# Modulation columns with two places and in written order on VectorE; low products last and U2 copied first in the passage to the up projection

## The chip, the core and the metric

The kernel runs on one core of a Trainium2 chip. The core has a matrix engine (TensorE, PE in the profile), three engines that work on vectors (VectorE or DVE, ScalarE or ACT, GpSimd or POOL), and SyncE (SP), which here only issues transfers. The engines run beside each other, each takes its own queue in order, and they wait for one another by semaphores. On-chip data lie in SBUF, the results of PE in PSUM. The metric is the time of one execution on the device in microseconds (us), lower is better.

## The reference, cut to what matters

One layer of a diffusion backbone is applied to 128 context tokens and 512 grid tokens; the kernel treats them as 640 columns of one matrix.

```python
def trunk_layer(x, cvec, lw, ...):
    mod = jax.nn.silu(cvec) @ lw['w_ada'] + lw['b_ada']            # 1024 -> 6 * 1024
    sh1, sc1, g1, sh2, sc2, g2 = jnp.split(mod, 6, axis=-1)
    h = rmsnorm(x, lw['norm1_g']) * (1.0 + sc1) + sh1
    mix, kh, vh, s_f, s_b = token_mixers(h, ...)     # short conv, HGRN2, attention, gMLP, gates, w_o
    x = x + g1 * mix
    h = rmsnorm(x, lw['norm2_g']) * (1.0 + sc2) + sh2
    x = x + g2 * conv_ffn(h, lw['w_up'], lw['ffn_conv_w'], lw['ffn_conv_b'], lw['w_down'])
    return x, kh, vh, s_f, s_b

def conv_ffn(h, w_up, cw, cb, w_down):
    z = dwconv3(h @ w_up, cw, cb)
    a, g = jnp.split(z, 2, axis=-1)
    return (jax.nn.silu(g) * a) @ w_down
```

`cvec` has two rows, one for the grid tokens and one for the context. All is float32. The result is `rmsnorm` of both outputs, with the keys, values and final HGRN2 states of the context.

## The kernel before

**Precision.** A float32 product is made of three passes of PE over a narrower type: each operand is split into a high half (a copy by ACT) and a low half (the rest, by a subtraction on DVE), and PE adds high times high, high times low and low times high. The weight of each product thus has a high and a low half, and so has the activation. Where `low_dma` is used, the low half is made by ACT (a negated copy) and an accumulating transfer that POOL issues.

**Order of the work.** Weight tiles go through a list of units; for each, the transfer is issued four units ahead, the split two ahead, and the products follow. Beside these run jobs, written as Python generators: HGRN2, gMLP, convolution, attention and the modulation columns. A clock of planned PE time counts up with each product (`tick`), and when a job's time has come it writes its next few instructions and yields how much planned time to wait; `drain` runs all jobs until a named result has been written. A planner then orders each engine's queue: among instructions whose inputs are ready by its own reckoning it takes the one written first, so an instruction that is ready early can be issued ahead of what was written before it. `tc.keep_in_program_order` ties an instruction behind the one written just before it for the same engine. In the gates in pairs and the up projection the switch `fixed` does that for all of DVE, ACT and POOL.

**Modulation.** Its first 16 blocks of 128 outputs are made by PE at the start. The other 32 are columns: `ada_cols` loads the 128 x 1024 weights of one block f (`w_adt`, 512 KB, L244) and DVE multiplies them with `silu(c)` of each of the two rows and sums along the way (L248, twice a column). Columns 16 to 39 run beside the mixer stage (g1, shift 2, scale 2), columns 40 to 47 beside the down projection (g2). Each column is loaded into the one region H, where its second multiplication also leaves its scraps, so a load waits for the column before it. `HD[4]` is the planned time between a load and its multiplications, `HD[5]` after each multiplication. No new column starts while HGRN2's tail is written, from "hgrn_out" to "hgrn_done"; in that tail PE transposes ten blocks (L648) and DVE multiplies each out of PSUM (L652).

**HGRN2 on DVE.** Seven levels of products, each with elementwise steps on DVE (L558, L544), copies on ACT (L510) and POOL, and small matmuls (L538). Weight splits of the mixer stage are L347/L348 and L334/L335.

**The passage to the up projection.** The up projection works in 22 pairs, each with seven products (`prod`, L1411) in a scheme that saves one of eight; product numbers and operands are in `PROD`. Product i takes 4 blocks of 128 with three passes, 12 matmuls. Products 1 and 2 of the first four pairs (`BRIDGE`, `up_start`) run while the second norm is finished (`norm2`); then `operands` makes the sums of activations for the others (operand 5 in region B, 6 in A, 7 in D, operand 3 in XL1) and `up_pair` carries on. Pairs 2 and 3 of the bridge get their low weights by `low_dma`. Products 6 and 5 of a pair go to two banks of one PSUM tile; product 6's bank is copied out by ACT (U2, `tmp`) before product 7 adds to it. All instructions of these helpers bear line L131, except matmuls.

**The down projection.** L1722 multiplies in two halves of 11 tiles; between them `down_out` scales with g2, and x from the stage before is read back into X0, X1 and G. Region X1 holds the convolution's results in the up projection; the last pair's are stored to `actd` from there.

Of the kernel before, what the change touches and what calls it, by code (L numbers as in the profile page):

```python
# [12 lines left out]
AF = mybir.ActivationFunctionType  # L13
# [1 line left out]
AX = mybir.AxisListType  # L15

P = 128
HD = [4, 5, 2.1, 7, 4.4, 1.4, 1.5, 5, 2.0, 2, 11]
NE = [lambda p, v: p, lambda p, v: v]
OUTS = 1  # L20
NPAIR = 22
BRIDGE = 4
# [7 lines left out]
HC = 320  # L30
# [20 lines left out]
def tile_step(ctx: ExitStack, tc: tile.TileContext, a: dict, outs: list, dbg=None):  # L51
# [178 lines left out]
    gcol = const.tile([P, 2, 2, 8], F32, name="gcol")  # L230
    growd = dram.tile([2, 16, P], F32, name="growd")

    def ada_cols(fs, tag="S0"):

        cr = region(tag, [P, 2, D])
        cf = cr.rearrange("p v c -> p (v c)")
        nc.sync.dma_start(cf, a["cc"].rearrange("v c -> (v c)").partition_broadcast(P))
        act(cf, cf, AF.Silu)
        for f in fs:
            while "hgrn_out" in R and "hgrn_done" not in R:  # L240
                yield 1
            raw = region("H", [P, D])
            junk = gp.tile([P, D], mybir.dt.bfloat16, tag="gt", name=nm("junk"))
            nc.sync.dma_start(raw, a["w_adt"][f - 16])  # L244
            yield HD[4]
            ar = sp.tile([P, 2], F32, tag="red", name=nm("ar"))
            for v in range(2):
                vec.scalar_tensor_tensor(raw if v else junk, raw, 1.0, cr[:, v], ALU.mult, ALU.mult,  # L248
                                         accum_out=ar[:, v:v + 1])
                yield HD[5]  # L250
            if f // 8 in (2, 5):
                vec.tensor_scalar(gcol[:, f // 8 // 5, :, f % 8], ar, p1[:, C_BADA + f:C_BADA + f + 1],
                                  None, ALU.add)
                if f % 8 == 7:
                    gain_rows(f // 8 // 5)
            else:
                modulate(f, ar)
        R["ada%d" % f] = True

    def gain_rows(i):  # L260

# [144 lines left out]
    def evac_in(sec, n, ps):  # L406
        psv = None if isinstance(ps, list) else ps[:, :, 0:HC]
        if sec in ("ff", "fb"):
            d = 0 if sec == "ff" else 1
            ff = need("A", "FF", [P, 2, 2, T])  # L410
            kk = need("B", "KK", [P, 2, 2, T])
            if psv is None:
                for c in range(2):
                    cs = slice(c * HC, (c + 1) * HC)
                    act(ff[:, d, n, cs], ps[c], AF.Sigmoid)
                    act(kk[:, d, n, cs], ps[c], AF.Sigmoid, scale=-1.0)
            else:
                act(c2(ff[:, d, n]), psv, AF.Sigmoid)
                act(c2(kk[:, d, n]), psv, AF.Sigmoid, scale=-1.0)
            i = d * 2 + n  # L420
            vec.tensor_scalar(ff[:, d, n], ff[:, d, n], oml[:, i:i + 1], lb[:, i:i + 1],
                              ALU.mult, ALU.add)
            vec.tensor_scalar(kk[:, d, n], kk[:, d, n], oml[:, i:i + 1], None, ALU.mult)
        elif sec == "q":
            dd = need("D", "HD", [P, 2560])
            act(c2(dd[:, n * T:(n + 1) * T]), psv, AF.Silu)
        elif sec == "g":
            o = need("MG1", "HO", [P, 2560])
            act(c2(o[:, 1280 + n * T:1280 + (n + 1) * T]), psv, AF.Silu)
        elif sec == "du":  # L430
            x0 = need("X0", "DX0", [P, 2560])
            act(c2(x0[:, n * T:(n + 1) * T]), psv, AF.Copy)
        elif sec in ("ac", "ax", "ab"):
            if (sec, n) == ("ac", 0):
                drain(lambda: "hgrn_out" in R)
            y = need("MG0", "YA", [P, 2, 2, T])
            if sec == "ac":
                act(c2(y[:, 0, n]), psv, AF.Copy)
                return
            if sec == "ab":  # L440
                drain(lambda: "conv" in R)
            x = y[:, 0 if sec == "ax" else 1, n]
            vec.tensor_tensor(c2(x), psv, c2(x), ALU.mult)
            if (sec, n) == ("ab", 1):
                R["ya"] = split_y("A", y[:, 1].rearrange("p n t -> p (n t)"))
        elif sec in ("ck", "cq", "cv"):
            if sec == "cv":
                dst = need("G", "CG", [P, 1280])[:, n * T:(n + 1) * T]
            else:
                f = need("F", "CF", [P, 2560])  # L450
                o = 0 if sec == "ck" else 1280
                dst = f[:, o + n * T:o + (n + 1) * T]
            sc = 0.125 if sec == "cq" else 1.0
            cg, cw = (4, 16) if sec == "cq" else (8, 8)
            dv = dst[:, 0:TS].rearrange("p (g r c) -> p r g c", g=cg, r=8)
            for (b, r0, r1) in ((0, 0, 5), (1, 5, 8)):
                src = ps[:, b, 0:(r1 - r0) * 64].rearrange("p (r g c) -> p r g c", g=cg, c=cw)
                act(dv[:, r0:r1], src, AF.Copy, scale=sc)
            act(dst[:, TS:T], ps[:, 1, 192:320], AF.Copy, scale=sc)
# [435 lines left out]
    def in_tile(sec, n, w):  # L895
        ps = pg()
        gemm(ps, w, 0, 8, xhk, xlk)
        evac_in(sec, n, ps)
        if n == 1:
            R[sec + "_done"] = True  # L900
        if n == 1 and sec in starts:
            start(starts[sec](), 1.5, SLACK[sec])
            if sec == "q":
                start(ada_cols(range(16, 40)), HD[7])

    def tok_tile(sec, kh, w):

# [493 lines left out]
            oact(c[:, i], x, AF.Copy)  # L1401
            low_dma(c[:, 2 + i].rearrange("p b c -> p (b c)"), x.rearrange("p b c -> p (b c)"))

    def prod(o, p_, i, first):
        u, ih, il = PROD[i]
        wh = up[p_, u][:, ih]
        wl = up[p_, "C" if i == 7 else u][:, il]
        xh_, xl_ = fx["x"][i]
        for k in range(4):
            for j, (w, x) in enumerate(((wh, xh_), (wh, xl_), (wl, xh_))):  # L1410
                mm(o, w[:, k, :], x[:, k, :], start=(first and k == 0 and j == 0),  # L1411
                   stop=(k == 3 and j == 2), skip_group_check=True)
            tick(0.44)

    def up_start(p_):

        if p_ == 2 or p_ == 3:
            up[p_, "b"] = [pm()[:, 0:HC], None]
        else:
            g = pg()  # L1420
            up[p_, "b"] = [g[:, 0, 0:HC], g[:, 1, 0:HC]]
        prod(up[p_, "b"][0], p_, 1, True)
        if p_ >= BRIDGE:
            first_copy(p_)
        b3 = up[p_, "b3"] = pm()[:, 0:HC]
        prod(b3, p_, 2, True)
        if p_ < BRIDGE - 1:
            first_copy(p_)
            first_sum(p_)
# [58 lines left out]

    S2 = ((0, 192, 321), (192, HC, 514))

    def up_pair(p_, r):


        n, q, o = p_ + 1, p_ - 1, p_ - 2
        inner, nx = p_ < NPAIR, n < NPAIR
        if o >= 0:
            taps(o, 1)
        if q >= 0:
# [30 lines left out]
        if q >= 0:  # L1529
# [7 lines left out]
            if p_ == 1:  # L1537
                first_copy(3)
                first_sum(3)
        if inner:  # L1540

            if up[p_, "b"][1] is None:
                up[p_, "b"][1] = pm()[:, 0:HC]
            b1, b2 = up[p_, "b"]
            prod(b1, p_, 6, False)
            oact(tmp(p_ % 2), b1, AF.Copy)
        if q >= 0:

            prod(up[q, "b"][1], q, 3, False)
# [5 lines left out]
        if nx:  # L1555
            up_bl(n)
        if inner:
            prod(b2, p_, 5, True)
            prod(b1, p_, 7, False)

# [32 lines left out]
    def up_all(_):  # L1593
        fx["x"] = {1: (hh[0][:, 0], hh[0][:, 1]), 2: (hh[0][:, 2], hh[0][:, 3])}
        r1 = {1: up_load1(1)}
        drain(lambda: "n2_2" in R)
        for p_ in range(BRIDGE):
            if p_ + 1 < BRIDGE:
                up_a(p_ + 1, r1[p_ + 1])
            if p_ + 2 < BRIDGE:  # L1600
                r1[p_ + 2] = up_load1(p_ + 2)
            up_start(p_)
            if p_ == 1:
                drain(lambda: "n2_3" in R)
                operands(0, 192)
            if p_ == 2:
                up_b(0)
                up_bl(0)
        drain(lambda: "n2_4" in R)
        r = {0: first}  # L1610
        operands(192, HC)
        operand3()
        r[1] = up_load(1)
        fixed[0] = True
        for p_ in range(NPAIR + 1):
            up_pair(p_, r)
        fixed[0] = False
        taps(NPAIR - 1, 1)
        gate(NPAIR - 1)
        gated(NPAIR - 1)  # L1620
        keep(NPAIR - 1)
        start(ada_cols(range(40, 48), "MG1"))

    units.append((lambda: None, lambda pr: up_first(), up_all))

# [65 lines left out]
    def down_tile(nh, kk_, ws):  # L1691
        if (nh, kk_) == (0, 3):
            x2[0:2] = [x2r("X0")[:, 0:1024], x2r("X0")[:, 1024:2048]]
            x2[4] = x2r("G")[:, 0:1024]
        if (nh, kk_) == (0, 10):
            x2[2:4] = [x2r("X1")[:, 0:1024], x2r("X1")[:, 1024:2048]]
        if kk_ == 0:
            if nh == 0:
# [10 lines left out]
                return  # L1709
            batch = acc["hold"]  # L1710
        last = kk_ == 10
        if (nh, kk_) == (0, 10):
            drain(lambda: "ada47" in R)
            grows["g2"] = gain_load(1, "S0")
        for t in range(5):

            halves = ((0, 256), (256, 512)) if nh == 1 and t == 4 else ((0, 512),)
# [284 lines left out]
```

## Time and profile before

| | |
|---|---|
| median of 3 runs | 1060.93 us (1059.95 to 1065.95) |
| profiled execution, its own time | 1062.54 us |
| its span, first to last instruction | 1060.8 us |
| mean granted PE clock | 0.987 |
| PE busy | 1030.6 us, 97% of the span |
| DVE busy | 795.8 us, 75% |
| ACT busy | 521.0 us, 49% |
| POOL busy | 119.3 us, 11% |

The stages by time from the span's start: modulation of the first norm and first sections to about 60 us; the other sections with HGRN2, convolution and attention to 315; gates to 560; output projection and second norm to 626, up projection to 906, down projection to the end. A line of the profile names the line of the kernel, the engine, the operation, and the tile written and read (`m<-XH,MG`: from XH and MG into m); in brackets stands how long the engine had been idle before, and what ended that. PE counts as busy while matmuls are in flight. The granted clock says which share of PE's full rate it was allowed.

### The profile page before, as it was taken

Reading aid. Unit: us, or ns where it says so; the run is one execution under the profiler, and the core shown is the slowest. Engines: PE = TensorE matmul, PEld = TensorE weight load, DVE = VectorE, ACT = ScalarE, POOL = GpSimd, SP = SyncE. Lnnn points to the kernel's source line nnn. Section 1 sums busy time; section 2 is a strip of 40 time slices with the busy share of each in tenths; the row PEclk is TensorE's granted clock in tenths of the full one; section 3 lists DMA queues with packets and bytes.
Section 4 is the critical chain, followed back from the end, with each engine's and each line's share of the span. In section 5 each row is a group of like instructions: output and inputs, shape, how many; then the busy total and the mean of one; then the engine's idle time right before and its main releaser. Section 6 shows DMA issues by size and latency. Waiting matters only on the chain.

```text
span 1060.8 us, 18792 instructions
## 1 busy us (share of the span) xinstructions
PE 1030.6 (97%) x7648; PEld 968.3 (91%) x7648; DVE 795.8 (75%) x1278; ACT 521.0 (49%) x890; POOL 119.3 (11%) x151
## 2 busy tenths in 40 slices
PE   7998999989999999999999998999999999999997
PEld 6698988989999999999998888999999999888886
DVE  6568698868877486776775787998888887776834
ACT  6252235324243354454453287777777677533532
POOL 1013011021100000000010022212211111000201
PEclk9998999999999999999999999999999999999999
DMA  9663433445226222422244268865666668984212
GB/s 373 230 218 104 123 106 114 128 128 167 76 75 216 73 92 83 150 69 81 90 154 144 100 178 169 197 163 145 154 159 162 171 153 217 354 287 159 80 40 100
DMA packets 53863, 158.73 MB, mean 150 GB/s; under 512 B 7792, under 2 KB 16400, under 8 KB 51728
## 3 DMA queue, kind: packets, MB, share of 16 engines
q1 hardware_dynamic: 42416, 132.47, 37.2%
q0 software_dynamic: 11360, 25.05, 11.2%
q8 instruction: 60, 0.98, 0.4%
q14 instruction: 27, 0.22, 0.1%
HBM read 126.80 MB, written 16.80 MB: 135 GB/s over the span
## 4 chain that ended last, share of the span: by engine, by line
PE 91%; DVE 3%; ACT 2%; DMA 2%; issue 1%; POOL 1%; SPq 0%; POOLq 0%; ACTq 0%; DVEq 0%
PE g L1411 20%; PE g L382 19%; PE m L1112 14%; PE g L1722 8%; PE m L1722 6%; PE m L1411 5%; PE g L1125 4%; PE m L1248 3%; PE g L1248 2%; PE g L924 1%; PE g L1824 1%; PE m L538 1%; PE m L211 1%; DMA MG<-raw 1%; PE m L864 1%
## 5 line engine op out<-in xcount | busy, mean ns | idle before, releaser
L382 PE MATMUL g<-XH,w 128*128 128x320 f32 x832 | 205.6, 321 | 0.0
L382 PEld LDWEIGHTS g<-XH,w 128*128 128x128 f32 x832 | 144.9, 191 | 3.8 <-issue 2.4
L382 PE MATMUL g<-XL,w 128*128 128x320 f32 x416 | 130.3, 313 | 0.0
L382 PEld LDWEIGHTS g<-XL,w 128*128 128x128 f32 x416 | 79.7, 192 | 0.2 <-issue 0.2
L335 DVE TENSOR_TENSOR w<-raw,w 128x1024 fp32r<-128x1024 f32 x34 | 41.5, 1221 | 18.0 <-ACT w L334 17.3
L334 ACT ACTIVATE w<-raw 128x1024 fp32r<-128x1024 f32 x34 | 35.8, 1053 | 24.5 <-PE g L1248 16.1
L1722 PE MATMUL g<-w,XH 128*128 128x512 f32 (+1 forms) x216 | 47.5, 372 | 0.0
L1722 PEld LDWEIGHTS g<-w,XH 128*128 128x128 f32 x216 | 38.5, 188 | 7.3 <-DVE X L131 0.2
L1112 PE MATMUL m<-XH,w 128*128 128x320 f32 x192 | 45.0, 309 | 0.0
L348 DVE TENSOR_TENSOR w<-raw,w 128x1024 fp32r<-128x1024 f32 (+1 forms) x29 | 41.4, 1426 | 3.9 <-ACT w L347 3.8
L347 ACT ACTIVATE w<-raw 128x1024 fp32r<-128x1024 f32 (+1 forms) x29 | 32.4, 1118 | 17.6 <-issue 6.6
L131 DVE SCALAR_TENSOR_TENSOR X<-MG,p2t,X 128x641 f32<-128x641 f32 x44 | 38.9, 884 | 2.1 <-ACT X L131 1.2
L1722 PE MATMUL m<-w,XH 128*128 128x512 f32 (+1 forms) x180 | 40.3, 368 | 0.0
L1722 PE MATMUL g<-w,XL 128*128 128x512 f32 (+1 forms) x180 | 40.1, 373 | 0.0
L248 DVE SCALAR_TENSOR_TENSOR junk<-H,S 128x1024 bf16<-128x1024 f32 x24 | 31.4, 1309 | 11.5 <-DMA H<-in_w_adt_dram 11.5
L131 DVE SCALAR_TENSOR_TENSOR X<-X,p2t,X 128x641 f32<-128x641 f32 x44 | 38.9, 884 | 1.2 <-ACT X L131 0.3
L1411 PE MATMUL g<-XL,C 128*128 128x320 f32 x240 | 38.7, 310 | 0.1
L1411 PE MATMUL g<-XL,w 128*128 128x320 f32 x240 | 38.8, 310 | 0.0
L1722 PEld LDWEIGHTS g<-w,XL 128*128 128x128 f32 x180 | 32.2, 188 | 6.8 <-DVE dt L1733 0.6
L1411 PEld LDWEIGHTS g<-XL,C 128*128 128x128 f32 x240 | 35.9, 188 | 1.0 <-ACT MG L131 0.8
L1411 PEld LDWEIGHTS g<-XL,w 128*128 128x128 f32 x240 | 35.9, 188 | 0.7 <-ACT MG L131 0.3
L1722 PEld LDWEIGHTS m<-w,XH 128*128 128x128 f32 x180 | 31.3, 189 | 5.3
(513 smaller groups left out, 2719.7 us busy)
## 6 DMA issues: line engine op xcount, KB each, us to landing
raw<-in_w_up_dram SPq DMA_DIRECT2D x35, 512.0 KB, 5.1
H<-in_w_adt_dram SPq DMA_DIRECT2D x32, 512.0 KB, 3.5
raw<-in_w_gp_dram SPq DMA_DIRECT2D x18, 640.0 KB, 3.9
raw<-in_w_in_dram SPq DMA_DIRECT2D x22, 512.0 KB, 4.4
raw<-in_w_down_dram SPq DMA_DIRECT2D x22, 512.0 KB, 3.6
actd<-X POOLq DMA_DIRECT2D x22, 320.5 KB, 5.4
G<-in_w_up_dram SPq DMA_DIRECT2D x11, 512.0 KB, 4.8
raw<-in_w_gate_dram SPq DMA_DIRECT2D x8, 640.0 KB, 3.9
```

Of the source, the lines that this page charges most:

```text
L131: r = f(*args, **kw)
L248: vec.scalar_tensor_tensor(raw if v else junk, raw, 1.0, cr[:, v], ALU.mult, ALU.mult, accum_out=ar[:, v:v + 1])
L334: act(w[0], raw, AF.Copy)
L335: vec.tensor_tensor(w[1], raw, w[0].bitcast(F32), ALU.subtract)
L347: act(w[:, 0], raw, AF.Copy)
L348: low = lambda: vec.tensor_tensor(w[:, 1], raw, w[:, 0].bitcast(F32), ALU.subtract)
L382: mm(o, w[:, h, k0 + k, :], r(k)[:, s], start=(k == 0 and i == 0), stop=(k == kt - 1 and i == 2))
L1112: mm(o, w[:, k, :], x[:, k, :], start=(first and k == 0 and j == 0), stop=(k == 3 and j == 2), skip_group_check=True)
L1125: mm(pb[:, c, 0:HC], w[:, h + k, :], y[:, x, k, s], start=(k == 0 and j == 0), stop=(k == 1 and j == 2))
L1248: mm(m, mh[k // 2][:, hx, k % 2, t * P:(t + 1) * P], wo[q][:, hw, k % 2, :], start=(k == 0 and i == 0), stop=(k == 7 and i == 2))
L1411: mm(o, w[:, k, :], x[:, k, :], start=(first and k == 0 and j == 0), stop=(k == 3 and j == 2), skip_group_check=True)
L1722: mm(acc[nh][t + c0 // 256][:, 0:c1 - c0], sl[k][hx][:, t * P:(t + 1) * P], w[:, hw, k, c0:c1], start=(kk_ == 0 and k == 0 and i == 0), st ...
```

## The change

1. A column's place is now chosen by a function, and there are two in turn. In the mixer stage even columns go to H; odd ones to the free half of DX0 (region X0) until HGRN2's totals are written, then to region A, which is free by then. In the down projection odd columns go to H and even ones to a part of region X1.
2. The next column's load is written before this column's multiplications. Both multiplications are tied behind what was written before them on DVE.
3. The planned time of a column is 2.2 (mixer) or 5 (down) after its multiplications, instead of 4.4 before them. The pause for HGRN2's tail is looked at after that time.
4. Before region A is used for the split of the convolution's result, all columns to 39 must have been written. In the down projection the drain for column 47 and the load of g2 stand ahead of x's reload into X1.
5. In the first four pairs the high weights' eight matmuls of products 1 and 2 come first, then the four of each with the low weights.
6. For pair 0, product 6 and its copy out (U2) are written ahead of operand 3's split, which is written in `up_pair` now, after the load of pair 1.

```diff
-HD = [4, 5, 2.1, 7, 4.4, 1.4, 1.5, 5, 2.0, 2, 11]
+HD = [4, 5, 2.1, 7, 2.2, 1.4, 1.5, 5, 2.0, 2, 11]
...
-    def ada_cols(fs, tag="S0"):
+    def ada_cols(fs, tag, homes, gap):
...
+        raws = {}
+
+        def load(f):
+            if f in fs and f not in raws:
+                raws[f] = homes(f)
+                nc.sync.dma_start(raws[f], a["w_adt"][f - 16])
+
+        load(fs[0])
+        yield HD[4]
         for f in fs:
-            while "hgrn_out" in R and "hgrn_done" not in R:
-                yield 1
-            raw = region("H", [P, D])
+            load(f + 1)
+            raw = raws.pop(f)
             junk = gp.tile([P, D], mybir.dt.bfloat16, tag="gt", name=nm("junk"))
-            nc.sync.dma_start(raw, a["w_adt"][f - 16])
-            yield HD[4]
             ar = sp.tile([P, 2], F32, tag="red", name=nm("ar"))
             for v in range(2):
-                vec.scalar_tensor_tensor(raw if v else junk, raw, 1.0, cr[:, v], ALU.mult, ALU.mult,
-                                         accum_out=ar[:, v:v + 1])
+                tc.keep_in_program_order(
+                    vec.scalar_tensor_tensor(raw if v else junk, raw, 1.0, cr[:, v], ALU.mult, ALU.mult,
+                                             accum_out=ar[:, v:v + 1]))
                 yield HD[5]
...
-        R["ada%d" % f] = True
+            yield gap
+            while "hgrn_out" in R and "hgrn_done" not in R:
+                yield 1
+        R["ada%d" % fs[-1]] = True
+
+    def col_home(f):
+
+        if f % 2 == 0:
+            return region("H", [P, D])
+        if "tots" not in R:
+            return need("X0", "DX0", [P, 2560])[:, 1280:1280 + D]
+        return need("A", "A2", [P, 2560])[:, 0:D]
...
             if (sec, n) == ("ab", 1):
+                drain(lambda: "ada39" in R)
                 R["ya"] = split_y("A", y[:, 1].rearrange("p n t -> p (n t)"))
...
-                start(ada_cols(range(16, 40)), HD[7])
+                start(ada_cols(range(16, 40), "S0", col_home, HD[4]), HD[7])
...
-    def prod(o, p_, i, first):
+    def prod(o, p_, i, first, part=None):
...
-        for k in range(4):
+        for k in range(4) if part is not None else ():
+            for j, (w, x) in enumerate(((wl, xh_),) if part else ((wh, xh_), (wh, xl_))):
+                mm(o, w[:, k, :], x[:, k, :], start=(first and not part and k == 0 and j == 0),
+                   stop=(part == 1 and k == 3), skip_group_check=True)
+                tick(0.147)
+        for k in range(4) if part is None else ():
...
-        prod(up[p_, "b"][0], p_, 1, True)
         if p_ >= BRIDGE:
+            prod(up[p_, "b"][0], p_, 1, True)
             first_copy(p_)
         b3 = up[p_, "b3"] = pm()[:, 0:HC]
-        prod(b3, p_, 2, True)
+        if p_ >= BRIDGE:
+            prod(b3, p_, 2, True)
+        else:
+            for part in range(2):
+                prod(up[p_, "b"][0], p_, 1, True, part)
+                prod(b3, p_, 2, True, part)
...
+    def up_u2(p_):
+
+        if up[p_, "b"][1] is None:
+            up[p_, "b"][1] = pm()[:, 0:HC]
+        b1 = up[p_, "b"][0]
+        prod(b1, p_, 6, False)
+        oact(tmp(p_ % 2), b1, AF.Copy)
+
     def up_pair(p_, r):
...
+        if p_ == 0:
+            up_u2(p_)
+            operand3()
...
-        if inner:
-
-            if up[p_, "b"][1] is None:
-                up[p_, "b"][1] = pm()[:, 0:HC]
-            b1, b2 = up[p_, "b"]
-            prod(b1, p_, 6, False)
-            oact(tmp(p_ % 2), b1, AF.Copy)
+        if inner and p_:
+            up_u2(p_)
...
         operands(192, HC)
-        operand3()
         r[1] = up_load(1)
...
-        start(ada_cols(range(40, 48), "MG1"))
+        def down_home():
+            if "col" not in fx:
+                fx["col"] = region("X1", [P, 2560])
+            return fx["col"][:, 0:D]
+
+        start(ada_cols(range(40, 48), "MG1", lambda f: region("H", [P, D]) if f % 2 else down_home(), 5))
...
         if (nh, kk_) == (0, 10):
+            drain(lambda: "ada47" in R)
+            grows["g2"] = gain_load(1, "S0")
             x2[2:4] = [x2r("X1")[:, 0:1024], x2r("X1")[:, 1024:2048]]
...
-        if (nh, kk_) == (0, 10):
-            drain(lambda: "ada47" in R)
-            grows["g2"] = gain_load(1, "S0")
```

1 line of the change is left out of this document (added).

## The prediction

> **What bounds the kernel now.** I read the page's busy line first, then the span cut into stages, then the waits of TensorE (PE), and only then single stretches in order of time. The page and three rows of the stages (columns: length, PE busy, PEld, DVE, ACT, POOL, granted clock, DMA share, GB/s):
>
> ```profile
> PE 1030.6 (97%) x7648; PEld 968.3 (91%) x7648; DVE 795.8 (75%) x1278; ACT 521.0 (49%) x890; POOL 119.3 (11%) x151
> ...
> 92.00:104.00 12.00, 9.15 (x55) 8.94 (x54) 10.59 (x16) 2.88 (x6) 1.68 (x1) 0.72 0.31 94
> 152.00:159.00 7.00, 5.05 (x98) 4.71 (x97) 7.00 (x12) 1.89 (x3) 1.15 (x1) 0.76 0.34 99
> 159.00:220.00 61.00, 61.00 (x668) 58.30 (x668) 49.73 (x102) 26.95 (x62) 11.60 (x10) 1.00 0.39 122
> 220.00:232.00 12.00, 8.03 (x48) 7.69 (x47) 8.85 (x21) 0.00 (x0) 0.00 (x0) 0.86 0.42 131
> 619.00:650.00 31.00, 25.54 (x161) 24.26 (x160) 25.29 (x43) 25.23 (x46) 10.22 (x23) 0.94 0.96 200
> ```
>
> PE is the bound. No PE work is removed by the change, so all it can do is fill or open holes in PE's time. Within the body of the kernel four stretches have holes: 2.85 us idle in 92-104, 1.95 in 152-159, 3.97 in 220-232 and 5.46 in 619-650. Each also costs clock: 12.00 x (1 - 0.72) = 3.4 us, 7.00 x 0.24 = 1.7, 12.00 x 0.14 = 1.7, 31.00 x 0.06 = 1.9. What ended the holes:
>
> ```profile
> PE m L648 <- DVE MG L652: 4.0, 1, 4.0
> PE g L924 <- ACT E L928: 2.9, 1, 2.9
> PE g L1411 <- ACT MG L131: 2.6, 1, 2.6
> PE m L538 <- issue: 1.9, 1, 1.9
> PE m L1411 <- DMA MG<-raw: 1.9, 1, 1.9
> ...
> DVE junk L248 <- DMA H<-in_w_adt_dram: 18.4, 13, 5.1
> ```
>
> Columns here: total, times, longest. The last line is VectorE's (DVE's): thirteen times its queue stood still because a modulation column (L248) had not landed in its one place, H.
>
> **The columns in the mixer stage.** The hole of 220-232, on DVE and then on PE:
>
> ```profile
> 222.07 1.22 DVE L348 TENSOR_TENSOR w<-raw,w 128x1024 fp32r<-128x1024 f32 x1
> 225.35 1.23 DVE L248 SCALAR_TENSOR_TENSOR junk<-H,S 128x1024 bf16<-128x1024 f32 x1 [2.06 <-DMA H<-in_w_adt_dram]
> ...
> 226.62 1.75 DVE L652 SCALAR_TENSOR_TENSOR MG<-m,p1t,MG 128x128 f32<-128x128 f32 x5
> ...
> 227.02 0.47 PE L648 MATMUL m<-cst,MG 128*128 128x128 f32 x1 [3.97 <-DVE MG L652]
> ```
>
> PE cannot make another transpose (L648) until L652 has emptied a PSUM buffer, and L652 sits behind a column that waits 2.06 us for its transfer and takes 1.23. With two places the next column is loaded one column ahead (L244 before L248), so the wait goes; with the denser pace (5.0 us of planned PE time a column, 2.2 + 2 x 1.4, for 7.2 before) the columns that were late here have run earlier, and between hgrn_out and hgrn_done no new one is written. If the weight split (222.07) stays in front, L652 starts at 223.3 for 226.62: 3.3 us. The clock then isn't lost; of its 1.7 us I take 1.4, since a short wait for L652's release (five tiles of two, 0.35 each) remains. Gain 4.7 us, bounds 0 and 3.97 + 1.7 = 5.7.
>
> [...]
>
> What it costs: more columns in the same time, and each tied behind what is written before it on DVE, so that none floats up into idle time. All DVE work in 130-205, then L248's share of it (columns: length, DVE busy and count, clock, DMA):
>
> ```profile
> 130.00:205.00 75.00, 67.73 (x137) 0.98 0.36 111
> ...
> 130.00:205.00 75.00, 22.18 (x36) 0.98 0.36 111
> ```
>
> The x36 are 18 multiplications with their accumulator reads, so 9 columns of 22.18 / 9 = 2.46 us, one each 8.3 us. At the written pace there would be 75 / 5.0 = 15: 6 more, 14.8 us, for 75 - 67.73 = 7.3 us of idle time. So DVE overruns by up to 7.5 us, and HGRN's DVE steps slip by that. The cover is PE's other tiles: in 159-220 PE is busy 61.00 of 61.00 us while DVE is busy for 49.73. I take 0 for it, and keep 0 and 7.5 for the range; if the cover goes, see the third rival.
>
> In 92-104 the hole ends with an ACT copy that waits for HGRN's L558 on DVE, with a column ahead of it:
>
> ```profile
> 74.14 1.23 DVE L248 SCALAR_TENSOR_TENSOR junk<-H,S 128x1024 bf16<-128x1024 f32 x1 [5.15 <-DMA H<-in_w_adt_dram]
> ...
> 89.37 2.87 DVE L248 SCALAR_TENSOR_TENSOR junk<-H,S 128x1024 bf16<-128x1024 f32 x1
> ...
> 96.78 0.83 ACT L510 ACTIVATE D<-B 128x640 f32<-128x640 f32 x1 [5.69 <-DVE B L558]
> ```
>
> The first column floated up to 74.14, when DVE had nothing else to do. Tied behind HGRN's first steps it comes later, and I take it to stand where the second stands here. So 0; bounds: no column in the chain, all of 2.85 + 3.4 = 6.2 us won, or a second pair with it, 2.46 lost. The 1.95 us of "issue" have no releaser that the change touches: 0. On the SP queue each load stands one column earlier, and the weight loads behind it wait less: 0. The second place is free space in DX0 and then in A; the drain before A is split again finds all columns done, unless they stay at 8.3 us each: 0.
>
> **The passage to the up projection.** PE, with what it waits for, then the other engines:
>
> ```profile
> 627.87 0.46 PE L1411 MATMUL m<-XH,MG 128*128 128x320 f32 x2
> 630.23 3.49 PE L1411 MATMUL m<-XH,MG 128*128 128x320 f32 x22 [1.90 <-DMA MG<-raw]
> 633.56 3.72 PE L1411 MATMUL m<-XH,w 128*128 128x320 f32 x24
> 637.97 0.41 PE L1411 MATMUL g<-A,E 128*128 128x320 f32 x1 [0.70 <-ACT A L131]
> 643.13 3.49 PE L1411 MATMUL g<-B,E 128*128 128x320 f32 x12 [2.55 <-ACT MG L131]
> ...
> 633.83 0.49 DVE L131 TENSOR_TENSOR MG<-m,s 128x320 f32<-128x320 f32 x1 [1.28 <-PE m L1411]
> 634.24 1.22 DVE L131 TENSOR_TENSOR E<-S,E 128x1024 fp32r<-128x1024 f32 x1
> ...
> 632.33 1.05 ACT L131 ACTIVATE E<-S 128x1024 fp32r<-128x1024 f32 x1
> 639.40 1.27 ACT L131 ACTIVATE XL<-X 128x1280 fp32r<-128x1280 f32 x1 [0.30 <-DVE X L131]
> 642.66 0.41 ACT L131 ACTIVATE MG<-g 128x320 f32<-128x320 f32 x1
> ...
> 637.65 1.29 POOL L131 DMA_DIRECT2D B<-X  x1 [1.24 <-DVE X L131]
> ...
> B<-X POOLq DMA_DIRECT2D x1, 256.0 KB, 5.0
> ```
>
> Low products last: pair 2 now has 16 products that need no low weight, at (633.56 - 630.23) / 22 = 0.15 us each 2.4 us, where it had 2. From 627.87 they reach 630.3, and the transfer landed at 630.2: the 1.90 us wait goes. But PE only comes sooner to the next wait, for the operand of product 6 in A (637.97). That chain shortens by what DVE loses at 633.83: pair 2 ends before DVE asks for it, so E's low half starts when ACT has its high half, 632.33 + 1.05 = 633.4, instead of 634.24; I take 0.9 (bounds 0 and 1.28). U2 copied first: product 5 waits for the copy of product 6's bank (642.66 + 0.41 = 643.07), which stands on ACT behind operand 3 and four other copies; now it runs at once. Then the low half of operand 5 decides: 637.65 + 5.0 = 642.65, or 641.75 with the 0.9. So product 5 starts 1.4 us earlier (bounds 0.5 and 1.9). Of the 1.9 us of clock I take 0.5: a hole of some 1.9 us remains, 1.90 lost no clock at 630, 1.95 did at 153. Operand 3 and the copies to C come 0.4 us or more later on ACT, with POOL's transfers for them; a later stall on their low halves, or on the next pair's sums on DVE, is the lower end, 0.5 lost. Sum 1.9 us, bounds -0.5 and 1.9 + 1.9 = 3.8.
>
> **The columns in the down projection.** Even columns now go to X1, which is free only when the last pair's output has been stored:
>
> ```profile
> 915.97 0.54 POOL L131 DMA_DIRECT2D actd<-X  x1 [12.46 <-DVE X L131]
> ...
> 919.62 1.23 DVE L248 SCALAR_TENSOR_TENSOR junk<-H,MG 128x1024 bf16<-128x1024 f32 x1 [3.21 <-ACT MG L238]
> 920.77 1.22 DVE L335 TENSOR_TENSOR w<-raw,w 128x1024 fp32r<-128x1024 f32 x1
> ...
> 928.78 5.60 PE L1722 MATMUL g<-w,XH 128*128 128x512 f32 x24
> ...
> raw<-in_w_down_dram SPq DMA_DIRECT2D x5, 512.0 KB, 6.2
> H<-in_w_adt_dram SPq DMA_DIRECT2D x2, 512.0 KB, 4.3
> actd<-X POOLq DMA_DIRECT2D x1, 320.5 KB, 5.9
> ```
>
> Store and load end at 915.97 + 5.9 + 4.3 = 926.2, 6.6 us after the first column's start of before, and SP's queue stands at that load meanwhile. Behind the column on DVE is a weight split (920.77) that I read as due at the tile of 928.78: 926.2 + 1.23 + 1.22 = 928.6, just in time. Later columns catch up, since two can be in flight; x2's reload into X1, now behind the drain, comes while PE works on the last tile of the first half and is asked for after it. I take 0, bounds 0 and 3.8: with 6.2 for store and load alike the split ends at 915.97 + 12.4 + 2.45 = 930.8, 2.1 late, and a hole can take 1.7 of clock.
>
> [...]
>
> **Sum.** 4.7 + 1.9 = 6.6 us. The profiled execution took 1062.54 us (span 1060.8), 1.6 above the median of 1060.93: it would become 1055.9, and the median 1054.3.
>
> **Rivals.** (1) The hole only moves: HGRN's tail slips on the fuller DVE, or a column is still in front of L652, and the 4.7 stay; the passage alone gives 1060.9 - 1.9 = 1059.0. For it: 7.3 us of idle time for up to 14.8 of work. Against: the 20 us before 220 have no PE hole.
> (2) The place in X1 comes late: 1054.3 + 3.8 = 1058.1. Against: DVE's later work has slack.
> (3) Slower: the denser columns on DVE in 130-205. It decides once PE runs out of tiles whose splits are ready: then the 7.5 us of overrun come through to PE, with two half-clock windows of 1.7 as in 92-104, and the hole of 220-232 stays: 1060.9 - 1.9 + 7.5 + 3.4 = 1069.9. Against: PE's 61.00 of 61.00.
> (4) Better: the column leaves the chain of 92-104: 1054.3 - 6.2 = 1048.1.
>
> **How the numbers follow.** The forecast has 0.50, with its own range 1051 to 1058; (1) 0.14, (2) 0.08, (3) 0.17, (4) 0.11. Half a per cent, 5.3 us, is about what a measurement tells from no change: faster is below 1055.6, slower above 1066.2. Of the forecast's 0.50, 0.36 lie below 1055.6: faster 0.36 + 0.11 = 0.47; same 0.14 + 0.14 + 0.08 = 0.36; slower 0.17. The range 1048 to 1066.5 leaves out most of (3) and part of (4), 0.17 together.
>
> **What would show it.** Right: no line for L648 waiting on L652 above 1 us, DVE's waits for columns near 0, the clock at 1.00 in 220-232, the wait on MG<-raw gone, product 5 right after operand 5's transfer. Wrong: waits of PE on DVE in 104-220, DVE idle before the first column in X1 with PE idle at the tile after it, or a new stall at the second pair of the up projection.

## The result and the profile after

The changed kernel took 1066.89 us in the median of 13 runs (1063.63 to 1069.14), the kernel before 1061.69 beside it (1059.67 to 1066.09, 13 runs): ratio 1.0042, 95% interval 1.0026 to 1.0057. By the ratio it is some 4.5 us slower (5.2 between the medians), less than half a per cent, where I had forecast 6.6 us less. It lies 0.4 us above my range.

The profiled execution took 1066.1 us with a span of 1064.3. Its busy line and four stretches of the span (columns as in the prediction: length, PE, PEld, DVE, ACT, POOL, granted clock, DMA share, GB/s):

```profile
PE 1034.0 (97%) x7648; PEld 970.4 (91%) x7648; DVE 790.8 (74%) x1278; ACT 520.5 (49%) x890; POOL 122.3 (11%) x151
...
130.00:159.00 29.00, 25.61 (x602) 23.94 (x601) 27.24 (x49) 11.41 (x23) 5.23 (x4) 0.89 0.41 129
220.00:232.00 12.00, 11.94 (x89) 11.48 (x88) 9.60 (x20) 4.28 (x7) 0.00 (x0) 1.00 0.42 146
300.00:372.00 72.00, 68.82 (x473) 67.37 (x472) 34.09 (x42) 24.95 (x31) 0.00 (x0) 0.98 0.34 113
619.00:660.00 41.00, 35.22 (x216) 33.45 (x215) 32.67 (x60) 32.85 (x65) 12.47 (x26) 0.92 0.89 194
```

The same stretches of before that the prediction did not show:

```profile
130.00:159.00 29.00, 26.87 (x616) 24.98 (x615) 27.70 (x47) 10.21 (x23) 4.66 (x4) 0.94 0.31 98
300.00:372.00 72.00, 72.00 (x509) 70.34 (x509) 44.29 (x64) 27.14 (x33) 0.00 (x0) 1.00 0.39 134
619.00:660.00 41.00, 35.39 (x226) 33.84 (x225) 33.74 (x56) 32.74 (x58) 11.93 (x25) 0.96 0.91 197
```

For each stretch I add PE's idle time and the clock that was lost (length times one minus the granted clock). 220-232: 3.97 + 1.68 before, 0.06 after, 5.6 us won. 130-159: 2.13 + 1.74 before, 3.39 + 3.19 after, 2.7 lost. 300-372: nothing before, 3.18 + 1.44 after, 4.6 lost. 619-660: 5.61 + 1.64 before, 5.78 + 3.28 after, 1.8 lost. Together 3.5 lost, as much as the spans differ (1064.3 and 1060.8). That is a match of the large pieces and no exact account: the first section's products began 2.1 us earlier in this execution (57.68 for 59.77), by chance in what precedes the change, and some 2 us more are spread over pieces too small to name.

So the hole that I had priced was closed, and a new one of nearly the same size had opened 120 us later. PE's waits after:

```profile
PE g L1436 <- DMA B<-X: 3.7, 1, 3.7
PE g L400 <- ACT gt L984: 3.2, 1, 3.2
PE g L943 <- ACT E L947: 3.1, 1, 3.1
...
PE m L557 <- issue: 1.5, 1, 1.5
...
PE m L557 <- DVE C L577: 1.1, 1, 1.1
```

The second line is the new one. It belongs to the gates: ACT makes a sigmoid (L984, L965 before) out of PSUM, and PE needs that place for the next product. ACT's queue there, in the kernel before:

```profile
343.46 0.80 ACT L965 ACTIVATE gt<-g,p1t 128x640 f32<-128x640 f32 x1 [5.78 <-PE g L382]
347.47 0.42 ACT L131 ACTIVATE H<-raw 128x256 fp32r<-128x256 f32 x1 [3.21 <-DMA raw<-in_w_gp_dram]
```

and in the changed kernel, with PE's row below:

```profile
345.37 0.42 ACT L131 ACTIVATE H<-raw 128x256 fp32r<-128x256 f32 x1 [9.54 <-DMA raw<-in_w_gp_dram]
345.70 0.78 ACT L984 ACTIVATE gt<-g,p1t 128x640 f32<-128x640 f32 x1
...
346.53 0.42 PE L400 MATMUL g<-XH,w 128*128 128x320 f32 x1 [3.18 <-ACT gt L984]
```

The two rows of ACT have changed places. `H<-raw` is the weight copy of the first of the gates in pairs (`g_a`), and its destination is the region H, the columns' old home. Before, the last column held H until 336.9 us, so the planner wrote the copy behind the sigmoid. Now the last column in H is done at 257.5, and the copy stands one place ahead. But its source, a weight transfer, lands at 345 to 347 us in either kernel. ACT stands 9.54 us before the copy, and the sigmoid behind it, which needed nothing any more (PE's last product before its wait had ended at 343.34), comes late, at 345.70. Of the columns' last ends in H, the row

```profile
L248 DVE DVE_READ_ACCUMULATOR H<-H,S x24: 73/81/95, 78.1 to 336.9; 128x1 f32 x24
```

is the group of before whose last start is 336.9; the one after is

```profile
L255 DVE DVE_READ_ACCUMULATOR H<-H,S x12: 72/81/92, 100.1 to 257.5; 128x1 f32 x12
```

That the planner moved the copy because H was free is my reading of these ends; its reckoning is in no profile, though the run with the old pace below agrees with it. That the copy's place makes the hole was tested.

### The profile page after: what moved, and what is told of

Its sections match the earlier page's. It is cut to its first block, busy times and chain, and to the rows that moved or that the text cites. A ratio compares the mean times of both kernels' runs of the same rounds, so it can differ in the third digit from the quotient of the medians.

```text
span 1064.3 us, 18792 instructions
## 1 busy us (share of the span) xinstructions
PE 1034.0 (97%) x7648; PEld 970.4 (91%) x7648; DVE 790.8 (74%) x1278; ACT 520.5 (49%) x890; POOL 122.3 (11%) x151
## 4 chain that ended last, share of the span: by engine, by line
PE 85%; DVE 5%; DMA 3%; ACT 2%; issue 2%; POOL 1%; SPq 0%; POOLq 0%; ACTq 0%; DVEq 0%
PE g L1436 20%; PE g L400 14%; PE m L1131 14%; PE g L1762 8%; PE m L1762 6%; PE m L1436 5%; PE g L1144 4%; PE m L1267 3%; PE g L1267 2%; PE g L943 1%; PE g L1864 1%; PE m L211 1%; DMA ycd<-C 1%; PE m L883 1%; DMA B<-X 1%
## 5 line engine op out<-in xcount | busy, mean ns | idle before, releaser
L1762 PE MATMUL m<-w,XL 128*128 128x512 f32 (+1 forms) x150 | 33.2, 368 | 0.0
```

The source lines that it names most:

```text
L1762: mm(acc[nh][t + c0 // 256][:, 0:c1 - c0], sl[k][hx][:, t * P:(t + 1) * P], w[:, hw, k, c0:c1], start=(kk_ == 0 and k == 0 and i == 0), st ...
```

## Experiments

Every comparison below is with the kernel before, run beside it on the same chip. The runs were made in four groups on four chips, so across groups I compare ratios. The first four runs asked whose the loss is.

**The columns alone.** All hunks of the diff but those of `prod`, `up_start`, `up_pair` and `operand3`.

> The change's columns alone (mixer stage and down projection), the passage to the up projection as before. Theory A: the slowdown lies in the mixer stage and the gates: the hole at L648 goes (-5 us), but column 39 ends early, region H is free early, and ACT's queue gets the first gate pair's copy into H ahead of a gate's sigmoid; it waits there for a weight transfer, PE idles 3.2 us and loses 1.7 us of clock. With some 3 us more lost around 140-160 this version is 3 to 5 us slower than before, and its profile shows the wait of PE on the gate's ACT line at about 343 us. Theory B (the passage is what costs): equal to before or up to 3 us faster.

Measured: 1066.27 us (before 1062.75), ratio 1.0026, interval 1.0008 to 1.0044. Theory A held: the loss is the columns', and the new wait of PE on the sigmoid (L984) is there with 3.0 us.

**The passage alone.** The hunks left out above, and no others.

> The passage alone (low products last in the first four pairs, U2 first), the columns as before. Theory A: within 1 us of before: the 1.90 us wait goes, but product 5 still waits for operand 5's low transfer, which lands no earlier. Theory B: 3 to 5 us slower than before.

Measured: 1060.95 us (before 1062.75), ratio 0.9984, interval 0.9969 to 1.0000. The median is 1.8 us lower, where theory A allowed 1; the interval does not quite tell that from nothing, and the trace has no such gain: the wait on MG<-raw went from 1.9 to 0.3 us, and in its place PE waits for operand 5.

```profile
PE g L1417 <- DMA B<-X: 3.3, 1, 3.3
...
PE m L1412 <- DMA MG<-raw: 0.3, 1, 0.3
```

**The first pair's copy on VectorE.** The changed kernel with one copy moved off ACT's queue; it still waits for the same transfer and writes the same place:

```diff
-        for b, x in zip(gw[p_, "br"], r):
-            oact(b[:, 0:2], x[:, 8:10], AF.Copy)
+        for i, (b, x) in enumerate(zip(gw[p_, "br"], r)):
+            if p_ == 0 and i == 1:
+                vec.tensor_copy(b[:, 0:2], x[:, 8:10])
+            else:
+                oact(b[:, 0:2], x[:, 8:10], AF.Copy)
```

> The changed kernel with one edit: the first gate pair's copy into H is made by DVE instead of ACT, so ACT's queue has nothing in front of the gate's sigmoid that waits for that transfer. Theory A: the hole of 3.2 us at 343 and its half-clock window go, 4 to 5 us faster than the changed kernel, about equal to before. Rival: the order of the planner shifts and a hole of the same size opens elsewhere, or PE waits for DVE instead; no gain over the changed kernel.

Measured: 1060.92 us (before 1062.75), ratio 0.9984, interval 0.9967 to 1.0001. Theory A held. The sigmoid is back to following PE at once, and the stretch is full:

```profile
343.00 0.80 ACT L984 ACTIVATE gt<-g,p1t 128x640 f32<-128x640 f32 x1 [5.72 <-PE g L400]
...
300.00:372.00 72.00, 72.00 (x510) 70.52 (x510) 37.32 (x48) 27.29 (x33) 0.00 (x0) 1.00 0.34 119
```

One copy's place on one queue was worth about 6 us (ratio 1.0042 against 0.9984), more than the whole loss and more than the 4 to 5 us that I expected.

**The old pace.** The changed kernel with `HD[4]` at 4.4 again. It is now the planned time ahead of the first column and, as `gap`, behind every column of the mixer stage, which makes 7.2 a column, as before the change.

> The changed kernel with HD[4] back at 4.4, so a column takes 7.2 us of planned time in the mixer stage, as before the change, with two places and written order kept. If the dense pace causes the waits at 142-153 (0.7 + 1.1 us, and a half-clock stretch twice as long as before's), they go: 2 to 4 us faster than the changed kernel. The hole at 343 stays in either case, since the copy into H still stands ahead of the sigmoid in ACT's queue; so slower than before by 1 to 3 us. If the pace is not the cause: the same time as the changed kernel within 1 us.

Measured: 1073.12 us (before 1062.75), ratio 1.0089, interval 1.0065 to 1.0114: slower still, and neither expectation held. The columns now reach into the attention's end, in written order:

```profile
303.32 1.22 DVE L255 SCALAR_TENSOR_TENSOR A<-A,S 128x1024 f32<-128x1024 f32 x1
...
306.97 1.22 DVE L255 SCALAR_TENSOR_TENSOR junk<-H,S 128x1024 bf16<-128x1024 f32 x1
...
308.31 1.08 DVE L863 TENSOR_SCALAR X<-X,ast 128x384 f32<-128x384 f32 x3
...
308.87 0.88 PE L866 MATMUL m<-cst,X 128*128 128x128 f32 x3 [4.63 <-DVE X L863]
```

The softmax that PE waits for stands behind two multiplications. So it is not the density alone that costs; a place where a tied column lands can have a price of its own.

The wait of PE on the sigmoid at 343, which I had expected to stay, is gone. The last column held H until 312.3 us in this run (257.5 in the changed kernel), and the sigmoid stands ahead of the copy again:

```profile
342.89 0.80 ACT L984 ACTIVATE gt<-g,p1t 128x640 f32<-128x640 f32 x1 [5.47 <-PE g L400]
...
351.52 0.42 ACT L131 ACTIVATE H<-raw 128x256 fp32r<-128x256 f32 x1 [5.55 <-DMA raw<-in_w_gp_dram]
```

That agrees with my reading that H, free early, let the copy move up. It is no proof, since this run moved much else as well.

**What holds the passage.** The four runs from here on keep the first pair's copy on VectorE. In the first, the second part of operand 5's low half is a subtraction on DVE:

```diff
-        split(x5, t5, True)
+        split(x5, t5, c0 == 0)
```

> Beside the first pair's copy on VectorE (that edit is kept in this and the next three), the second part of operand 5's low half is formed by VectorE (one 128x512 subtraction, 0.68 us by the rows of the other operands) and not by the accumulating transfer. My theory: the passage did not get shorter because that transfer, issued 1.2 us earlier, took 6.0 to 6.5 us instead of 5.0 with operand 7's issued right behind the one before it; without it PE's wait of 3.2 us on B<-X goes, product 5 follows within 1 us behind the copy of the product before it, and the time falls by 1.5 to 3.9 us, to 1057.0 to 1059.4 (with the half-clock window behind the hole gone as well: the upper gain). Rival: the next operand is late instead (PE then waits on D<-X by 2 us or more, since its transfer lands only 1.4 us before product 7 now), and the time stays at 1060.4 to 1061.4.

Measured: 1059.59 us (before 1062.46), ratio 0.9967, interval 0.9947 to 0.9986, 0.2 us above the first theory's range. Both theories are half right. The wait on B is gone, and the next operand is late by 2.2 us:

```profile
635.91 2.02 PE L1439 MATMUL g<-B,E 128*128 128x320 f32 x12 [0.90 <-ACT MG L131]
...
640.30 0.38 PE L1439 MATMUL g<-D,E 128*128 128x320 f32 x1 [2.22 <-DMA D<-X]
```

PE's waits for product 5 and product 7 sum to 3.1 us, so most of the 3.2 us moved on. The ratio is 0.0017 lower than without this edit (1.8 us, overlapping intervals). The profiled execution has the clock at 1.00 in 619-650 where the run before this edit had 0.94, but it is the fastest of the twelve, 2.9 us below their median, so it does not show that the edit's gain is clock.

**Columns slow, then dense.**

```diff
-            yield gap
+            yield 2 * gap if f < 24 else gap
```

> The run before this one, and in addition the pause behind each of the first eight columns is doubled (4.4 instead of 2.2), the other sixteen keep 2.2. Theory: 130 to 159 us of the changed kernel lost 1.3 to 1.6 us of TensorE and a half-clock window because the denser columns bring the rows of gains to 142 us, where TensorE waits 0.7 us for them, and hold VectorE at the C copies (1.1 us): they go back to about 165 us, PE is busy 26.8 of 29 again as before, and the time is 1.0 to 2.0 us below the run before this one; no PE wait on DVE at 300 to 318, where the pace of 4.4 for all 24 columns cost 4.6 + 2.3 us. Rival: whatever moves the columns' end moves the planner's order elsewhere, and a new wait of 2 us or more appears after 220; then it is equal or slower by up to 6.

Measured: 1061.96 us (before 1062.46), ratio 0.9988, interval 0.9967 to 1.0010: the theory missed, the rival held. In 130-159 PE was busy for 27.37 of 29 us (25.70 in the run before) with the clock at 1.00, as the theory had it. But the rows of gains at 161.7 made PE wait 2.0 us where they had cost 0.7, and on ACT another copy now stands ahead of a sigmoid and waits for a step of DVE, which itself waits for a transfer. How the later columns brought that about is not shown:

```profile
PE g L400 <- ACT gt L984: 2.0, 1, 2.0
PE m L281 <- DVE gcol L259: 2.0, 1, 2.0
...
329.14 1.27 ACT L1056 ACTIVATE X<-B 128x1280 fp32r<-128x1280 f32 x1 [7.53 <-DVE B L1041]
330.31 0.78 ACT L984 ACTIVATE gt<-g,p1t 128x640 f32<-128x640 f32 x1
```

**Two places, no written order.** `keep_in_program_order` around L255 is taken off.

> The changed kernel with the first pair's copy on VectorE, the columns free of the written order on VectorE (both places and the pace kept). Theory: the second place is what removed the wait for H and with it the hole of 3.97 us at 223; the written order only fixes where a column stands, and without it the time stays within 1.0 us of 1060.9 with PE busy 11.9 of 12 in 220 to 232. Rival: the written order is what keeps the columns out of the way of the product that PE waits for there; then PE is at 8 to 10 of 12 us in that stretch, and the time is 2 to 4 us above.

Measured: 1061.03 us (before 1062.46), ratio 0.9977, interval 0.9958 to 0.9996. The rival held at 220: there PE had to wait 5.2 us, longer than before the change, since with two places five multiplications and a weight split in a row, none of them waiting, stood in front of the product out of PSUM (L670, L652 before). First and last of the multiplications, and the wait:

```profile
216.23 1.22 DVE L254 SCALAR_TENSOR_TENSOR junk<-A,S 128x1024 bf16<-128x1024 f32 x1
...
222.78 1.23 DVE L254 SCALAR_TENSOR_TENSOR junk<-A,S 128x1024 bf16<-128x1024 f32 x1
...
224.05 1.27 DVE L670 SCALAR_TENSOR_TENSOR MG<-m,p1t,MG 128x128 f32<-128x128 f32 x4
...
224.45 0.48 PE L666 MATMUL m<-cst,MG 128*128 128x128 f32 x1 [5.19 <-DVE MG L670]
```

So the second place, at this pace, does not close that hole by itself; the written order is needed (the order with one place was not run). But the time did not rise: with free columns and two places another hole, at 92, is closed, which the free columns with one place had in the kernel before:

```profile
92.00:104.00 12.00, 12.00 (x93) 12.00 (x92) 12.00 (x19) 3.20 (x6) 0.76 (x1) 1.00 0.46 138
```

**Low products last, product 6 not first.** The lines of the diff in `up_pair` and `up_all` that move `up_u2` and `operand3` are undone; `prod` in two parts stays.

> The changed kernel with the first pair's copy on VectorE, product 6 with its copy put back where it was (in the pair's body), operand 3 ahead of it as before; low products last is kept. Theory: low products last takes away the wait of 1.9 us on MG<-raw, and product 6 first gains nothing, because product 5 waits for its operand's transfer either way: the time is within 0.8 us of 1060.9, the wait on B<-X or on the copy in front of product 5 sums to 3 to 4 us in both. Rival: product 6 first is worth the 1.4 us that I forecast and low products last nothing: then this run is slower by 1.0 to 2.0 us.

Measured: 1061.97 us (before 1062.46), ratio 0.9988, interval 0.9964 to 1.0012, and not to be told from 0.9984 with product 6 first. By the medians it is 1.1 us above 1060.9, just outside the theory's 0.8 and inside the rival's range, by the ratios 0.4, so the time decides for neither. In the trace the wait on MG<-raw stays away, and the wait in front of product 5 changed its name and kept its size:

```profile
642.65 0.64 PE L1439 MATMUL g<-B,E 128*128 128x320 f32 x1 [3.53 <-ACT MG L131]
```

**Written order where it helps.** From these runs: the order is good at 220 and bad at 92. With the copy and operand 5 as above:

```diff
-                tc.keep_in_program_order(
-                    vec.scalar_tensor_tensor(raw if v else junk, ...))
+                i = vec.scalar_tensor_tensor(raw if v else junk, ...)
+                if f >= 24:
+                    tc.keep_in_program_order(i)
```

> The run with operand 5's low half on VectorE (first pair's copy on VectorE too), and the written order only for columns 24 to 39; columns 16 to 23 are placed freely again. Theory: the written order is what removes the stall of 4 to 5 us at 220 (5.2 us without it), but it also leaves the one of 3.1 us at 90 with its half clock, which the free columns did not have (TensorE 12.00 of 12 us at clock 1.00 in 92 to 104, against 10.24 at 0.72 in the written order). With each where it helps, both go: TensorE over 11.8 of 12 in 92 to 104 and in 220 to 232, and the time 2.5 to 5.0 us below that run's 1059.6. Rival: free columns run ahead and cost at the convolution's products instead (2.6 us of waits at 127 to 149 in the free version, half clock 0.88 in 130 to 159), so the stage keeps its length: within 1.0 us of 1059.6.

Measured: 1052.36 us (4 runs, 1051.44 to 1053.47; before 1062.58), ratio 0.9899, interval 0.9880 to 0.9918. This beats both kernels, by 10.2 us the one before. It is 7.2 us below the run with operand 5's edit, 2.2 more than the theory's upper end. The two profiled executions differ by only 3.3 us, since that of the other run was its fastest. Both holes are closed:

```profile
92.00:104.00 12.00, 12.00 (x94) 12.00 (x93) 12.00 (x19) 3.19 (x6) 0.76 (x1) 1.00 0.40 132
130.00:159.00 29.00, 27.82 (x710) 26.01 (x698) 26.56 (x46) 13.79 (x25) 7.47 (x6) 0.94 0.28 91
220.00:232.00 12.00, 12.00 (x85) 11.34 (x84) 9.53 (x17) 6.12 (x16) 0.00 (x0) 1.00 0.53 157
```

> The same with the written order for columns 32 to 39 alone. Theory: the columns that stood in front of the queries' products at 216 to 224 in the free version are the last eight, so this gives the same as the run before this one, within 0.8 us. Rival: columns 24 to 31, free, run ahead and push the last eight against that place again; then a wait of 3 us or more on VectorE at 218 to 225 is back, and the time is 2 to 5 us above the run before this one.

With `f >= 32`: 1054.00 us (5 runs; before 1062.58), ratio 0.9916, interval 0.9899 to 0.9933. No wait at 220 either, so it is the last eight columns that have to be tied there. The 1.6 us to the run before are twice what I allowed, inside overlapping intervals. In 130-159 PE was busy for 26.40 us at 0.88 here and for 27.82 at 0.94 in the run before: it waited 1.5 us there for DVE's step L578. Those are products of HGRN2's levels (L558), not the convolution's, as the expectation ahead of the last one calls them.

> The kernel before with the passage's part of the change and operand 5's low half on VectorE, nothing of the columns. Theory: once the gates' stall is avoided the columns' part is worth nothing (its gain of 4 to 5 us at 220 is given back over 140 to 300), so this equals the run with all three, 1058.6 to 1060.6, with the stall of 3.9 us at 222 still there and no wait on B<-X. Rival: the columns' part is worth 2 us or more without the gates' stall; then this run is at 1061.5 or above.

The kernel before with the passage's hunks and operand 5's edit: 1060.70 us (before 1062.58), ratio 0.9987, interval 0.9972 to 1.0002. It is just above the theory's 1060.6 and below the rival's 1061.5, with the wait of 3.9 us at 222 still there. The columns in full written order, with the gates mended, are worth some 2 us by the ratios (0.9967 with them), which the overlapping intervals do not tell from nothing.

> The changed kernel with the written order for columns 24 to 39 only, and nothing else: the first pair's copy is on ScalarE again, operand 5's low half by the transfer. Theory: the stalls are separate and add up. Freeing the first eight columns is worth what it was beside the other two edits (1059.6 to 1052.4, 7.2 us), so this is at 1066.9 - 7.2 = 1059.7, 1058 to 1061, with the gates' stall of about 3 us and its half clock still there (ScalarE's copy for the first pair stands ahead of the sigmoid) and 56.5 us of gates become 61. Rival: with the columns done earlier everything in front of the gates is earlier too, and the copy's raw transfer is there in time: then no stall, gates of 56.5 us, and 1053 to 1056.

The changed kernel with the order from column 24 and nothing else: 1056.24 us (9 runs, 1053.39 to 1059.51; before 1061.98), ratio 0.9947, interval 0.9926 to 0.9967. That lies between the two theories' ranges, but the trace decides for the first one: the stall at the gates is there, smaller.

```profile
334.44 0.42 ACT L131 ACTIVATE H<-raw 128x256 fp32r<-128x256 f32 x1 [8.43 <-DMA raw<-in_w_gp_dram]
334.76 0.78 ACT L985 ACTIVATE gt<-g,p1t 128x640 f32<-128x640 f32 x1
```

What remains of it there is 2.1 us with the clock at 1.00. That may be part of why this came out 3.5 us better than 1059.7, but the profiled execution took 1053.63, 2.6 us less than the median.

## Why the prediction was wrong

**The hole of 220-232 (4.7 us): right in its place and nearly in its size**, 5.6 won; no wait of L666 (L648 before) on L670 is left, DVE no longer waits for a column in the mixer stage (11.5 us in 6 of the 13 waits before; the other 7 were in the down projection, where one of 4.0 us is left). The reason I gave was only half of it: I named the second place, the denser pace and the pause from hgrn_out to hgrn_done; with all three, but free of the written order, PE's wait there grew to 5.2.

**The step that failed is the term for the columns' places, put at 0.** I asked what each column waits for and who waits for a column, and wrote that the second place is free space and the drain before A finds all columns done: 0. I did not ask who takes H next. H is handed from the last column to the gates' first copy, and freeing it 80 us earlier let that copy, by my reading of the traces, pass a sigmoid on ACT. That is the 4.6 us of 300-372 that made a kernel of about 1061 one of 1067. With that copy off ACT's queue the change is worth some 1.7 us by the ratio (0.9984, with an interval that reaches 1.0001) and not 6.6; the rest lies in the next terms. My list of what would show me wrong had waits of PE on DVE in 104-220; it had nothing on ACT.

**"The columns' pace costs 0, the cover is PE's other tiles": too low.** PE did stay at 61.00 of 61.00 in 159-220. But the cost came in 130-159, the front part of the stretch that I had counted over: 2.7 us, with the rows of gains now made at 142 (PE waits 0.7) and a product of HGRN2's levels at 149 that waits for its step on DVE (L577, 1.1) among the columns. That is the slip of HGRN's steps that I had named, at a third of the 7.5 us. The third rival had PE run out of tiles with ready weight splits; here it waited for these steps instead. With the first eight columns slower both waits left 130-159.

**"92-104: 0": right, for a reason I had wrong.** I took the first column to come later, and it did: it stood at 74.1 and stands at 95.1, behind the HGRN steps that it had delayed. By rival (4) that should have won up to 6.2 us. The hole stayed, 3.07 for 2.85, since ACT makes it:

```profile
90.75 0.78 ACT L529 ACTIVATE D<-B 128x640 f32<-128x640 f32 x1 [9.99 <-DVE B L577]
...
92.38 0.36 ACT L947 ACTIVATE E<-g 128x256 f32<-128x256 f32 x1
92.79 0.58 PE L943 MATMUL g<-w,XH 128*128 128x256 f32 x1 [3.07 <-ACT E L947]
```

PE waits for E, and E stands behind a copy to D that waits 9.99 us. In the first run with the order from column 24, four copies to E have gone by before that copy to D (first and last shown):

```profile
90.67 0.39 ACT L948 ACTIVATE E<-g 128x256 f32<-128x256 f32 x1 [0.82 <-PE g L944]
...
96.79 0.39 ACT L948 ACTIVATE E<-g 128x256 f32<-128x256 f32 x1 [1.97 <-PE g L944]
99.34 0.83 ACT L530 ACTIVATE D<-B 128x640 f32<-128x640 f32 x1 [2.17 <-DVE B L578]
```

It looks like the gates' stall once more: one queue, two instructions in the wrong order. No run moved that copy alone; but PE is busy for 20.00 of 20 us in 84-104 in all four runs that leave the first eight columns free, and the wait of 3.1 us is in every run of the changed kernel that ties them.

**The passage (1.9 us): mis-sized; in the trace it is nothing or a loss.** Low products last did what I wrote (the wait on MG<-raw is gone in the changed kernel), product 6 started earlier. The term "product 5 starts 1.4 us earlier, because operand 5's transfer ends at 641.75" failed. I let the transfer be issued earlier and last the same. In the changed kernel:

```profile
639.65 1.29 POOL L131 DMA_DIRECT2D B<-X  x1 [2.19 <-ACT B L131]
...
646.30 3.27 PE L1436 MATMUL g<-B,E 128*128 128x320 f32 x11 [3.66 <-DMA B<-X]
...
B<-X POOLq DMA_DIRECT2D x1, 256.0 KB, 6.5
```

The stage's work stands 3.2 us later here, so it was issued 1.2 us earlier (637.65 before); but it took 6.5 us for 5.0, and so landed no earlier. Operand 7's first transfer now goes out 1.5 us behind operand 5's first one, where 3.6 us lay between them before. That one delays the other is my reading, not shown alone: with the old order and the columns changed the transfer took 5.6 us, in the seven traces that have it in the new order 5.8 to 6.5, and taking it away removed the wait and left most of it to the next operand. The 0.5 us of clock that I expected to win became 1.6 lost (0.92 for 0.96 of 41 us).

**The down projection (0): right.** The first column in X1 came at 931.0 (926.2 forecast, DVE idle 4.0 us before it), and PE had no hole.

**The clock: not to be read from a hole's length here.** In 130-159 the granted clock was 0.89 with no hole over 1.54 us in the changed kernel, and 0.94 with a longest hole of 1.2 us in the first run with the order from column 24. In the passage, with a hole of 3.66 us that ended at 646.30, 0.50 was granted in 646-650.

## What to carry to other kernels

When a change frees a buffer earlier, ask who takes the buffer next and on which queue. Here, by my reading, the planner moved that instruction up; it then stood 9.54 us waiting for a weight transfer, and PE waited 3.18 us for the sigmoid behind it on ACT. A transfer that is issued earlier into a busy stretch need not end earlier by as much: here it went out 1.2 us earlier by the stage's work, with a DMA share of 0.89 in 619-660, took 6.5 us for 5.0 and landed no earlier. A tie to the written order is no property of a job as a whole; here it was right for the last third of the columns and wrong for the first, and choosing by column was worth some 7 us by the ratios.

## What the runs showed that was not expected

The same hole does not always cost the same clock. In 84-104 PE was busy for 16.9 of 20 us, with one hole of 3.1 us, in three executions of nearly the same order: the columns alone, the changed kernel, and operand 5's edit.

```profile
84.00:104.00 20.00, 16.92 (x108) 16.73 (x108) 16.08 (x17) 2.93 (x6) 5.40 (x3) 0.74 0.20 63
```

```profile
84.00:104.00 20.00, 16.93 (x120) 16.74 (x120) 16.02 (x20) 4.47 (x8) 3.71 (x3) 0.83 0.26 79
```

```profile
84.00:104.00 20.00, 16.93 (x126) 16.73 (x126) 16.93 (x20) 4.48 (x8) 4.10 (x3) 0.91 0.24 79
...
130.00:159.00 29.00, 25.70 (x651) 23.76 (x652) 27.70 (x50) 11.67 (x24) 5.19 (x4) 1.00 0.41 126
```

The clock lost is 5.2, 3.4 and 1.8 us. In 130-159 the last of them lost none with waits of 1.1 and 1.3 us at L557, where the changed kernel lost 3.2 us with 1.1 and 1.5. So several microseconds between executions of one kernel may be of this kind, though no kernel here was traced twice, and one trace does not price a hole's clock.
